# Block 1's loads in another order, attention's last product for two query tiles at a time, and the last tile's norm on VectorE

## The chip, the cores and the metric

The kernel runs on one core of one Trainium2 chip. The metric is the time of one execution in device microseconds (us). A core has TensorE (PE: matrix products; PEld is its loading of weights), VectorE (DVE), ScalarE (ACT), GpSimd (POOL) and SyncE (SP), which here issues all DMAs. Each engine runs its own instructions in the order in which they were written, and waits for others by semaphores. Products are summed up in PSUM, which has 8 banks of 128 x 512 fp32.

## The reference

One decoder layer for 512 positions of width 1024, in fp32, with a condition vector c. All of it is computed:

```python
c_act = silu(c)
sh1, sc1, g1, sh2, sc2, g2 = split(c_act @ ada_w + ada_b, 6)
h = x * (1 + sc1) + sh1
q, k, v, z, xbc, dt = split(h @ w_in, ...)       # w_in 1024 x 4112
o_attn = attention of 8 heads x 64, causal, with a distance penalty
xs, B, C = split(silu(conv4(xbc)))
y = state space scan of 16 heads x 64, gated by silu(z), normed in 2 groups
x = layer_norm(alpha * x + (1 + g1) * (concat(o_attn, y) @ w_out))
h = x * (1 + sc2) + sh2
x = layer_norm(alpha * x + (1 + g2) * conv_ffn(h))   # 1024 -> 2 x 2816 -> 1024
```

## The kernel before

**Precision.** A large product is made of three products of fp32r parts: a tensor `w` is split into a rounded part `wh` (ACT copies it) and the rest `wl` (DVE subtracts), and h into `hh` and `hl`; then wh·hh, wl·hh and wh·hl are summed up in one bank. So for each 512 KB slab `raw` of weights there is one ACT step of 128x1024 (`wh`) and one DVE step (`wl`), and 24 PE products of 512 columns for a tile `fm` (8 blocks of 128 input columns x 3).

**Order of the work.** The kernel is written as some dozens of generators ("threads") with priorities. A planner (class `Order`) takes, step by step, the thread whose next operation could start first by modelled prices, and writes it to its engine. Buffers come from pools with quotas (`buf`, `bank`, `R.limit`); a thread that finds no buffer, or whose `Need(...)` is not marked, stands back. So a change in one thread moves operations of others on all engines. Almost all operations are recorded at line 300 of the profile, inside the planner; the names of tiles tell them apart.

**The start.** h is made in eight blocks of 128 columns (k = 0 to 7). `start_load` issues, on SP, for each block the 256 KB of x (`xk`), a slab of w_in (`wr`, 384 KB) and the columns of ada_w that give the block's shift and scale (`aw`, four DMAs of 256 KB). SP's DMAs rotate over eight semaphores, so a ninth waits for the landing of the first. `start_acc` sums aw times silu(c) over the eight kc on DVE, in two halves that are added at the end (`acc`); `start_h` sums that over the partitions with one-column products on PE (`pa`). A few kc can be left to PE instead: KPE says how many, each then one product of `aw` with `csil` for the shift and one for the scale (the trace counts two instructions for each). From `pa` come `mod` (DVE), then `hh` and `hk` (ACT, from the transposed x, `px`) and `hl` (DVE). `products` keeps six banks (`first`) over all eight blocks, 18 products of 512 columns each; until block 0's hh is there it fills PE with products of the identity (`first<-ident`). Behind block 7 stand 16 products `pd`, then the tiles `fm` of q, k, x and v. ACT and DVE take the four-step convolutions of the six `first` banks (`Y`, `BT`, `CT`: ACT one step, DVE three, of 511, 510 and 509 columns), which frees these banks for fm. Next, with the scan's own steps (`pcs`, `pxt`, `pst`, `py`, `pyo` on PE; `xe`, `csb`, `xd`, `st`, `Y` on DVE), comes attention.

**Attention.** `attention(j)` runs for four pairs of heads, j = 0 to 3, and four query tiles of 128, t = 0 to 3. A unit (j, t, i) makes scores `psS` (PE), maximum (`mx`, DVE), exponentials and scaling of `pr` (ACT, DVE), transposes (`pT`, PE) and copies back to pr. `att_pv` then makes, for each tile t, 2(t+1) products `pov` of pr and V in one bank of the pair; each writes 64 of 128 partitions. The buffers pr are four.

**The end.** `ln2` takes the norm of one of four tiles, in parts as the down product's banks `dn` are done: y, XN (DVE), statistics, then 1/sqrt as a POOL `pow` on one column (mv), `center` (subtract the mean, times gain) and the scale step (times 1/sqrt, plus bias), each one DVE operation; `side` does the same for the last 256 columns with ACT and two POOL operations. Each part has its own DMA to the output.

Of the kernel before, what the change touches and what calls it, by code (L numbers as in the profile page):

```python
# [12 lines left out]
OP = mybir.AluOpType  # L13
# [3 lines left out]
P = 128  # L17
SEQ = 512
DM = 1024
NT = SEQ // P  # L20
KC = DM // P
# [383 lines left out]
def layer_kernel(  # L405
# [13 lines left out]
    out2 = out[0]  # L419
# [119 lines left out]
    NF = 768  # L539
    AW, XK, WR, ACC, WF = {}, {}, {}, {}, {}  # L540

    KPE = {0: 2, KC - 1: 4}

    def start_load():
        for k in range(KC):
            c0 = k * P

            def rows():
                xk = yield buf("s", [P, NT, P], "xk")
                yield S.dma_start(xk, x2[:, c0:c0 + P].rearrange("(t p) f -> p t f", p=P))  # L550
                XK[k] = xk
                R.mark(("x", k))
                wr = yield buf("b", [P, NF], "wr", "raw")
                yield S.dma_start(wr, w_in[k * P:(k + 1) * P, 3328:4096])
                WR[k] = wr
                R.mark(("sl", k))

            if k:
                yield from rows()
            aw = AW[k] = yield buf("e", [P, 2, KC, P], "aw")  # L560
            for k0 in (0, 4):
                for s in range(2):
                    yield S.dma_start(aw[:, s, k0:k0 + 4], ada[k0 * P:(k0 + 4) * P, s * DM + c0:s * DM + c0 + P]
                                      .rearrange("(k p) n -> p k n", p=P))
                R.mark(("aw", k, k0))
            if not k:
                yield from rows()
        R.mark("loads")
        WR["dt"] = yield buf("s", [P, KC, 16], "wdr")
        yield S.dma_start(WR["dt"], w_in[:, 4096:4112].rearrange("(k p) n -> p k n", p=P))  # L570
        R.mark("wdr")

    def start_acc():
        yield Need("csil")
        for k in range(KC):
            acc = yield buf("s", [P, 2, 2, P], "acc")
            n = KC - KPE.get(k, 0)
            for kc in range(n):
                if kc % 4 == 0:
                    yield Need(("aw", k, kc))  # L580
                a_, q = acc[:, kc % 2], AW[k][:, :, kc, :]
                if kc < 2:
                    yield V.tensor_scalar(a_, q, csil[:, kc:kc + 1], None, op0=OP.mult)
                else:
                    yield V.scalar_tensor_tensor(a_, q, csil[:, kc:kc + 1], a_, op0=OP.mult, op1=OP.add)
            yield V.tensor_add(acc[:, 0], acc[:, 0], acc[:, 1])
            if n == KC:
                R.free(AW[k])
            ACC[k] = acc
            R.mark(("acc", k))  # L590
# [34 lines left out]
    def start_h():  # L625
        for k in range(KC):
            yield Need(("acc", k), ("aw", k, 4), "ada_b")
            acc, n = ACC[k], KPE.get(k, 0)
            pa = yield bank("mix", "pa")
            for s in range(2):  # L630
                yield T.matmul(pa[:, s:s + 1], acc[:, 0, s], ones[:, 0:1], start=True, stop=not n)
                for kc in range(KC - n, KC):
                    yield T.matmul(pa[:, s:s + 1], AW[k][:, s, kc], csil[:, kc:kc + 1], start=False, stop=kc == KC - 1)
            if n:
                R.free(AW[k])
            R.free(acc)
            mod = yield buf("t", [P, 2], "mod")
            yield V.scalar_tensor_tensor(mod[:, 1:2], pa[:, 1:2], 1.0, adab[:, 8 + k:9 + k], op0=OP.add, op1=OP.add)
            yield V.tensor_add(mod[:, 0:1], pa[:, 0:1], adab[:, k:k + 1])
            R.free(pa)  # L640
            hk = yield buf("s", [P, SEQ], "hk")
            yield Need(("px", k))
            yield A.activation(hh[:, k], PX[k], AF.Identity, bias=mod[:, 0:1], scale=mod[:, 1:2])
            R.mark(("hh", k))
            yield A.activation(hk, PX[k], AF.Identity, bias=mod[:, 0:1], scale=mod[:, 1:2])
            R.free(PX[k], mod)
            R.mark(("hk", k))
            yield V.tensor_sub(hl[:, k], hk, hh[:, k].bitcast(F32))
            R.free(hk)
            R.mark(("h", k))  # L650
# [314 lines left out]
                R.spawn(att_unit(j, t, i), 4)  # L965

    def att_pv(j, po):
        for t in range(NT):
            yield Need(("pT", j, t, 0), ("pT", j, t, 1))
            yield [T.matmul(po[i * 64:i * 64 + 64, t * P:(t + 1) * P],  # L970
                            VT[b // 2][:, b % 2, (2 * j + i) * 64:(2 * j + i + 1) * 64],
                            PRT[j, t][:, i, b * P:(b + 1) * P], start=(b == 0), stop=(b == t))
                   for b in range(t + 1) for i in range(2)]
            R.free(PRT.pop((j, t)))
        if j % 2 == 0:
            OA[j] = yield buf("e", [P, 2, 2, SEQ], "oa", dt=F32R)
        o = OA[j - j % 2][:, j % 2]
# [281 lines left out]
    def ln2(t, ps, cuts):  # L1259
# [28 lines left out]
        def center(c0, c1):  # L1288
            return V.scalar_tensor_tensor(r[:, c0:c1], r[:, c0:c1], mv[:, 0:1], lg2[:, c0:c1],
                                          op0=OP.subtract, op1=OP.mult)  # L1290

        yield center(*cut[0])
        yield V.scalar_tensor_tensor(mv[:, 3:4], mv[:, 0:1], -1.0, mv[:, 2:3], op0=OP.mult, op1=OP.mult)
        R.spawn(side(cut[-1][1]), 0)
# [292 lines left out]
```

## Time and profile before

| | |
|---|---|
| median of 3 runs | 733.77 us (732.68 to 734.45) |
| profiled execution | 734.33 us, its span 732.6 us |
| PE busy | 717.2 us (98%), granted clock 0.989 on the mean |
| DVE, ACT, POOL busy | 526.4 us (72%), 316.6 us (43%), 60.3 us (8%) |
| bytes read and written | 96.20 MB and 2.13 MB |

The profile tells of one execution: for each engine what it ran and when, and what released it from a wait. The span runs from its first to its last instruction, the rest of the execution's time lies around it. A time like 62.92 is counted from the span's start. In a timeline, PE's duration column holds a modelled pipeline end and is longer than a product's share; the distance of two starts is what a product costs.

### The profile page before, as it was taken

How to read it: one execution, taken by the hardware profiler on the slowest of the kernel's cores; microseconds unless marked ns; L12 is line 12 of the kernel's file. 1: busy time of each engine (PE TensorE's matmuls, PEld its weight loads, DVE VectorE, ACT ScalarE, POOL GpSimd, SP SyncE). 2: the span in 40 equal slices, each digit the busy share in tenths (PEclk: the TensorE clock that was granted, in tenths of full speed). 3: DMA queues.
4: the chain of work that ended last, by engine and by line, in shares of the span. 5: the costliest groups of instructions: out<-in, count | busy, mean ns of one | idle time of the engine just before them, and what ended most of it. 6: DMA issues, size and time to landing. Idle time of an engine off the chain costs nothing.

```text
span 732.6 us, 9614 instructions
## 1 busy us (share of the span) xinstructions
PE 717.2 (98%) x3623; PEld 585.3 (80%) x3623; DVE 526.4 (72%) x929; ACT 316.6 (43%) x526; POOL 60.3 (8%) x70
## 2 busy tenths in 40 slices
PE   8999999999999999999999999999999999999995
PEld 8777777788777788888998888888888888888884
DVE  4888999999898999776865887655656664227246
ACT  2436576663576633332753444444444452212100
POOL 0010102000000001000100000000000009300023
PEclk8999999999999999999999999999999999999998
DMA  9995487453254755232633543332333144323202
GB/s 255 299 258 172 120 231 220 136 165 92 56 167 121 244 210 176 75 101 85 173 88 114 165 152 91 109 88 87 97 105 87 60 159 168 102 87 90 83 30 86
DMA packets 115831, 98.95 MB, mean 135 GB/s; under 512 B 5325, under 2 KB 97865, under 8 KB 115785
## 3 DMA queue, kind: packets, MB, share of 16 engines
q1 hardware_dynamic: 115785, 98.34, 45.1%
q8 instruction: 28, 0.46, 0.3%
q14 instruction: 18, 0.15, 0.1%
HBM read 96.20 MB, written 2.13 MB: 134 GB/s over the span
## 4 chain that ended last, share of the span: by engine, by line
PE 82%; DMA 6%; DVE 6%; ACT 3%; SPq 1%; issue 1%; POOL 1%; POOLq 0%; ACTq 0%; DVEq 0%
PE up L300 34%; PE dn L300 17%; PE fm L300 12%; PE po L300 9%; PE first L300 3%; DMA csb<-drcs 2%; SPq L300 1%; ACT csb L300 1%; PE psS L300 1%; PE pov L300 1%; DMA raw<-in_mix_in_w_dram 1%; PE pT L300 1%; DVE acc L300 1%; DMA aw<-in_ada_w_dram 1%; DVE wl L300 1%
## 5 line engine op out<-in xcount | busy, mean ns | idle before, releaser
L300 DVE TENSOR_TENSOR wl<-raw,wh 128x1024 fp32r<-128x1024 f32 x102 | 128.0, 1256 | 88.7 <-ACT wh L300 86.0
L300 ACT ACTIVATE wh<-raw 128x1024 fp32r<-128x1024 f32 x102 | 106.8, 1051 | 88.3 <-PE dn L300 54.6
L300 PE MATMUL up<-h2h,wh 128*128 128x512 f32 (+1 forms) x384 | 144.7, 377 | 0.0
L300 PE MATMUL up<-h2l,wh 128*128 128x512 f32 (+1 forms) x384 | 144.0, 375 | 0.0
L300 PE MATMUL up<-h2h,wl 128*128 128x512 f32 (+1 forms) x384 | 143.9, 375 | 0.0
L300 PE MATMUL dn<-wh,mid 128*128 128x512 f32 (+1 forms) x356 | 102.5, 371 | 0.0
L300 DVE SCALAR_TENSOR_TENSOR u<-up,fprm,u 128x511 f32<-128x511 f32 x88 | 65.8, 749 | 35.4 <-ACT u L300 33.9
L300 PEld LDWEIGHTS up<-h2h,wl 128*128 128x128 f32 x384 | 72.2, 188 | 14.7
L300 PEld LDWEIGHTS up<-h2h,wh 128*128 128x128 f32 x384 | 72.1, 188 | 14.1
L300 PEld LDWEIGHTS up<-h2l,wh 128*128 128x128 f32 x384 | 72.1, 188 | 14.0
L300 PEld LDWEIGHTS dn<-wh,mid 128*128 128x128 f32 x356 | 64.6, 188 | 12.6
L300 PE MATMUL fm<-hh,wh 128*128 128x512 f32 x176 | 73.9, 420 | 0.0
L300 PE MATMUL fm<-hl,wh 128*128 128x512 f32 x176 | 69.3, 394 | 0.0
L300 PE MATMUL fm<-hh,wl 128*128 128x512 f32 x176 | 69.3, 394 | 0.0
L300 PE MATMUL dn<-wl,mid 128*128 128x512 f32 (+1 forms) x178 | 66.1, 371 | 0.0
L300 ACT ACTIVATE u<-up,fprm 128x512 f32<-128x512 f32 x44 | 34.2, 778 | 51.3 <-PE up L300 51.3
L300 POOL TENSOR_TENSOR XN<-XN,l 128x512 f32<-128x512 f32 x16 | 25.0, 1580 | 244.5 <-ACT l L300 243.8
L300 PE MATMUL po<-wh,os 128*128 128x512 f32 x128 | 41.7, 394 | 0.0
L300 PEld LDWEIGHTS fm<-hh,wl 128*128 128x128 f32 x176 | 33.1, 188 | 7.9
L300 PEld LDWEIGHTS fm<-hh,wh 128*128 128x128 f32 x176 | 33.2, 188 | 7.7 <-issue 1.7
L300 PEld LDWEIGHTS dn<-wl,mid 128*128 128x128 f32 x178 | 33.5, 188 | 6.3
L300 DVE SCALAR_TENSOR_TENSOR acc<-ad,csil,acc 128x1024 f32<-128x1024 f32 x28 | 36.7, 1309 | 2.3 <-DMA ad<-in_ada_w_dram 2.2
(227 smaller groups left out, 1069.2 us busy)
## 6 DMA issues: line engine op xcount, KB each, us to landing
raw<-in_ffn_up_w_dram SPq DMA_DIRECT2D x44, 512.0 KB, 4.4
ad<-in_ada_w_dram SPq DMA_DIRECT2D x32, 512.0 KB, 4.8
raw<-in_mix_in_w_dram SPq DMA_DIRECT2D x26, 512.0 KB, 6.1
raw<-in_ffn_down_w_dram SPq DMA_DIRECT2D x22, 512.0 KB, 4.0
aw<-in_ada_w_dram SPq DMA_DIRECT2D x32, 256.0 KB, 5.9
raw<-in_mix_out_w_dram SPq DMA_DIRECT2D x12, 512.0 KB
csb<-drcs SPq DMA_DIRECT2D x8, 512.0 KB, 5.5
wr<-in_mix_in_w_dram SPq DMA_DIRECT2D x8, 384.0 KB
```

What stands on the lines that cost most here:

```text
L300: getattr(self.hw[op.eng], op.fn)(*op.args, **op.kw)
```

## The change

It has three parts. The first: in `start_load`, block 1's `xk` and `wr` are issued behind its `aw` and no longer ahead of it (block 0 had that order already); and of the kc that PE took, the four of block 7 go to DVE, so that only block 0 leaves two to PE. The second: `att_pv` waits for two query tiles, issues the products of both in one group and frees both buffers behind it. The third: `ln2` of the last tile makes its three parts (512, 256 and 256 columns) on DVE, all three `center` steps and then the three scale steps with a DMA behind each; ACT's and POOL's steps of `side` and the DVE operation that made mv's fourth column are left out there.

```diff
-    KPE = {0: 2, KC - 1: 4}
+    KPE = 2
@@ start_load
-            if k:
+            if k > 1:
                 yield from rows()
...
-            if not k:
+            if k < 2:
                 yield from rows()
@@ start_acc
-            n = KC - KPE.get(k, 0)
+            n = KC - KPE if k == 0 else KC
@@ start_h
-            acc, n = ACC[k], KPE.get(k, 0)
+            acc, n = ACC[k], 0 if k else KPE
@@ att_pv
-        for t in range(NT):
-            yield Need(("pT", j, t, 0), ("pT", j, t, 1))
+        for t0 in range(0, NT, 2):
+            ts = (t0, t0 + 1)
+            yield Need(*(("pT", j, t, i) for t in ts for i in range(2)))
             yield [T.matmul(po[i * 64:i * 64 + 64, t * P:(t + 1) * P],
...
-                   for b in range(t + 1) for i in range(2)]
-            R.free(PRT.pop((j, t)))
+                   for t in ts for b in range(t + 1) for i in range(2)]
+            R.free(*(PRT.pop((j, t)) for t in ts))
@@ ln2
+        if last:
+            cut = cuts
+            for c in cut:
+                yield center(*c)
+            for c0, c1 in cut:
+                q = r[:, c0:c1]
+                yield V.scalar_tensor_tensor(q, q, mv[:, 2:3], lb2[:, c0:c1], op0=OP.mult, op1=OP.add)
+                yield S.dma_start(out2[t * P:(t + 1) * P, c0:c1], q)
+            R.free(mv)
+            return
```

The planner moves other operations with these, on all engines, from the start to the middle of the output projection; behind it the orders are the same until the last tile. Three places follow, each as it stands in before and behind the change. The numbers in the names count buffers and differ between the two.

SP at the start, from the first DMA on; aw_98 is block 0's, xk_121, wr_128 and aw_132 are block 1's in before, aw_121, xk_139 and wr_144 behind the change:

```order
 L300 DMA xk_111<-in_x_dram 128x4x128
 L300 DMA wr_117<-in_mix_in_w_dram 128x768
-L300 DMA xk_121<-in_x_dram 128x4x128
-L300 DMA wr_128<-in_mix_in_w_dram 128x768
-L300 DMA aw_132<-in_ada_w_dram 128x4x128 x4
+L300 DMA aw_121<-in_ada_w_dram 128x4x128 x4
+L300 DMA xk_139<-in_x_dram 128x4x128
+L300 DMA wr_144<-in_mix_in_w_dram 128x768
```

The four aw DMAs moved ahead of the x and the slab of the same block; all other DMAs of the start stand as they stood.

DVE behind block 7, in before: hl of block 7, the first four wl, and the convolutions; first_102 is the bank that BT frees:

```order
L300 TENSOR_TENSOR hl_95<-hk_601,hh_94 128x512
L300 TENSOR_TENSOR wl_609<-raw_390,wh_608 128x1024
L300 TENSOR_TENSOR wl_622<-raw_439,wh_621 128x1024
L300 TENSOR_TENSOR wl_633<-raw_488,wh_632 128x1024
L300 TENSOR_TENSOR wl_659<-raw_535,wh_658 128x1024
L300 SCALAR_TENSOR_TENSOR Y_657<-first_99,prm_76,Y_657 128x511
L300 SCALAR_TENSOR_TENSOR BT_654<-first_102,prm_76,BT_654 128x511
L300 SCALAR_TENSOR_TENSOR BT_654<-first_102,prm_76,BT_654 128x510
L300 SCALAR_TENSOR_TENSOR BT_654<-first_102,prm_76,BT_654 128x509
```

and behind the change:

```order
L300 TENSOR_TENSOR hl_95<-hk_606,hh_94 128x512
L300 TENSOR_TENSOR wl_612<-raw_391,wh_611 128x1024
L300 TENSOR_TENSOR wl_625<-raw_437,wh_624 128x1024
L300 TENSOR_TENSOR wl_636<-raw_486,wh_635 128x1024
L300 SCALAR_TENSOR_TENSOR BT_648<-first_102,prm_76,BT_648 128x511
L300 SCALAR_TENSOR_TENSOR BT_648<-first_102,prm_76,BT_648 128x510
L300 SCALAR_TENSOR_TENSOR BT_648<-first_102,prm_76,BT_648 128x509
```

The fourth wl and the step of Y moved behind BT's three steps (the fourth wl by some 20 rows); on ACT the fourth wh moved likewise, behind the first steps of Y, BT and CT.

PE in the first head pair's attention, in before, from the transposes of tile 0's second head on (pT and pov of pr_1367 are tile 0's, of pr_1368 tile 1's):

```order
L300 MATMUL pT_1429<-ident_68,pr_1367 128x128
L300 MATMUL fm_1353<-hh_94,wh_1076 128x512
L300 MATMUL fm_1353<-hl_95,wh_1076 128x512
L300 MATMUL fm_1353<-hh_94,wl_1077 128x512
L300 MATMUL pT_1442<-ident_68,pr_1368 128x128 x2
L300 MATMUL pf_1444<-ident_68,fr_1428 128x96
L300 MATMUL pov_1366<-pr_1367,V_1351 64x128 x2
L300 MATMUL fm_1353<-hh_94,wh_1076 128x512
...
L300 MATMUL pov_1366<-pr_1368,V_1351 64x128 x4
L300 MATMUL psS_1492<-qk_767 128x512
```

and behind the change (pr_1334 is tile 0's, pr_1335 tile 1's):

```order
L300 MATMUL pT_1462<-ident_68,pr_1335 128x128 x2
L300 MATMUL fm_1445<-hh_94,wh_1105 128x512
L300 MATMUL fm_1445<-hl_95,wh_1105 128x512
L300 MATMUL fm_1445<-hh_94,wl_1106 128x512
L300 MATMUL pT_1472<-ident_68,pr_1336 128x128 x3
L300 MATMUL pov_1333<-pr_1334,V_1317 64x128 x2
L300 MATMUL pov_1333<-pr_1335,V_1317 64x128 x4
L300 MATMUL pT_1475<-ident_68,pr_1336 128x128 x3
```

The products of both tiles stand side by side, behind tile 1's last transposes. Over the whole kernel the groups of pov fall from 16 to 8.

## Rows read from the trace of the kernel before

**Rows 1.** The page: busy time, share of the span and instructions of each engine; and the chain of work that ended last, by engine.

```profile
PE 717.2 (98%) x3623; PEld 585.3 (80%) x3623; DVE 526.4 (72%) x929; ACT 316.6 (43%) x526; POOL 60.3 (8%) x70
PE 82%; DMA 6%; DVE 6%; ACT 3%; SPq 1%; issue 1%; POOL 1%; POOLq 0%; ACTq 0%; DVEq 0%
```

**Rows 2.** Busy time in six stretches. The columns: stretch, its length, busy us and instructions of each engine, the granted clock of PE (1.00 is 2.4 GHz), DMA share, GB/s.

```profile
17.00:50.00 33.00, 31.57 (x153) 25.01 (x151) 28.86 (x77) 13.13 (x18) 0.00 (x0) 1.00 1.09 289
50.00:62.00 12.00, 11.99 (x58) 10.03 (x59) 6.87 (x14) 6.64 (x10) 2.50 (x12) 0.86 0.99 286
62.00:138.00 76.00, 73.45 (x408) 57.12 (x407) 71.24 (x138) 49.55 (x118) 9.71 (x9) 1.00 0.57 162
138.00:262.00 124.00, 123.64 (x765) 97.58 (x765) 113.80 (x279) 72.65 (x153) 4.75 (x8) 1.00 0.49 152
262.00:724.00 462.00, 462.00 (x2175) 381.72 (x2173) 293.46 (x395) 169.33 (x222) 39.41 (x31) 1.00 0.35 107
724.00:732.60 8.60, 0.11 (x1) 0.00 (x0) 4.37 (x10) 0.60 (x1) 3.23 (x4) 0.69 0.28 102
```

**Rows 3.** PE's waits between 58 and 724 us, three of six kinds: who waited, for whom, us in total, times, longest.

```profile
PE py L300 <- ACT csb L300: 0.6, 1, 0.6
PE pst L300 <- DVE xe L300: 0.6, 2, 0.4
PE pT L300 <- DVE pr L300: 0.5, 1, 0.5
```

**Rows 4.** Timeline of PE at the start: start, duration, operation, count.

```profile
11.99 4.19 PE L300 MATMUL first<-ident 128*128 128x128 f32 x18
15.97 1.06 PE L300 MATMUL px<-ident,xk 128*128 128x128 f32 x4
16.68 1.89 PE L300 MATMUL first<-hh,whf 128*128 128x512 f32 x6
18.40 1.53 PE L300 MATMUL first<-hh,wlf 128*128 128x512 f32 x6
```

**Rows 5.** Timeline around blocks 6 and 7: a DVE row, then PE from the second eight one-column products on.

```profile
49.52 0.88 DVE L300 SCALAR_TENSOR_TENSOR acc<-aw,csil,acc 128x256 f32<-128x256 f32 x2
...
52.73 1.03 PE L300 MATMUL pa<-csil,aw 128*128 128x1 f32 x8
53.62 0.94 PE L300 MATMUL first<-hh,whf 128*128 128x512 f32 x3
54.40 2.44 PE L300 MATMUL first<-hh,wlf 128*128 128x512 f32 x6
...
58.75 1.56 PE L300 MATMUL first<-hh,whf 128*128 128x512 f32 x6
60.14 1.53 PE L300 MATMUL first<-hh,wlf 128*128 128x512 f32 x6
...
62.92 0.39 PE L300 MATMUL pd<-hh,wdt 128*32 128x512 f32 x1
```

**Rows 6.** Timeline behind block 7: ACT, then DVE, then PE's first fm.

```profile
59.15 1.06 ACT L300 ACTIVATE wh<-raw 128x1024 fp32r<-128x1024 f32 x1 [0.75 <-DMA raw<-in_mix_in_w_dram]
...
61.99 0.78 ACT L300 ACTIVATE Y<-first,prm 128x512 f32<-128x512 f32 x1
62.67 0.77 ACT L300 ACTIVATE BT<-first,prm 128x512 f32<-128x512 f32 x1
...
60.24 1.23 DVE L300 TENSOR_TENSOR wl<-raw,wh 128x1024 fp32r<-128x1024 f32 x1 [0.59 <-ACT wh L300]
62.02 1.23 DVE L300 TENSOR_TENSOR wl<-raw,wh 128x1024 fp32r<-128x1024 f32 x1 [0.56 <-ACT wh L300]
63.16 0.75 DVE L300 SCALAR_TENSOR_TENSOR Y<-first,prm,Y 128x511 f32<-128x511 f32 x1
63.82 2.31 DVE L300 SCALAR_TENSOR_TENSOR BT<-first,prm,BT 128x511 f32<-128x511 f32 x3
...
66.60 0.39 PE L300 MATMUL fm<-hh,wh 128*128 128x512 f32 x1
```

**Rows 7.** Timeline of PE around two groups of pov, of the first head pair's tiles 0 and 1.

```profile
138.99 0.44 PE L300 MATMUL pov<-pr,V 128*64 128x128 f32 x4
139.36 0.50 PE L300 MATMUL fm<-hh,wh 128*128 128x512 f32 x1
139.70 0.39 PE L300 MATMUL fm<-hl,wh 128*128 128x512 f32 x1
...
141.54 0.40 PE L300 MATMUL fm<-hh,wl 128*128 128x512 f32 x1
141.87 0.66 PE L300 MATMUL pov<-pr,V 128*64 128x128 f32 x8
142.46 0.50 PE L300 MATMUL psS<-qk 128*128 128x512 f32 x1
```

**Rows 8.** Timeline of the tail: DVE, then POOL.

```profile
725.87 0.74 DVE L300 SCALAR_TENSOR_TENSOR XN<-XN,mv,RW 128x512 f32<-128x512 f32 x1
...
727.79 1.34 DVE L300 SCALAR_TENSOR_TENSOR XN<-XN,mv,RW 128x256 f32<-128x256 f32 x2
...
726.03 0.99 POOL L300 TENSOR_TENSOR mv<-mv,half 128x1 f32<-128x1 f32 x1 [1.50 <-DVE mv L300]
727.93 1.79 POOL L300 TENSOR_TENSOR XN<-XN,RW 128x256 f32<-128x256 f32 x2 [0.91 <-ACT XN L300]
```

## The prediction

> **What bounds the kernel now.** I read the page first, then the stretches, then PE's waits, then the timelines of the places that the change touches. [rows 1]: PE is busy 98% of the span and holds 82% of the chain that ended last, so on the whole only what shortens PE's work, or lets PE start it earlier, is worth anything. [rows 2] shows where that is not the whole story. From 262 to 724 PE is busy in all 462.00 us, and what arrives earlier there leaves earlier by as much. From 138 to 262 it is busy 123.64 of 124.00 us, with DVE at 92%. From 62 to 138 PE is busy 73.45 of 76.00 us and DVE 71.24 of 76.00 (94%): two engines near their ends, and the one gains nothing without the other. [rows 3] lists waits of PE after 58 us; three kinds of 0.5 to 0.6 us, all on the chains of DVE and ACT in that stretch. The last 8.6 us have no PE work but one matmul: a chain on DVE, POOL and the output's DMA. Only this tail, PE's path until 62 us and the switches of PE in attention are what the change can move.
>
> **Part 1, the order of the loads and the last block's sums.** *Block 1.* In before, PE makes 18 filler products (11.99 to 15.97), then block 1's transposition, and starts block 0 at 16.68 [rows 4]. Behind the change 14 of these products stand there (7 pairs in place of 9), and the transposition comes after the seventh product of block 0. 14 x 0.221 = 3.1, so block 0 starts at 15.1, 1.6 us earlier. This is an upper end: the first six products of block 0 take 1.72 us (16.68 to 18.40), 287 ns each, where the last 12 of block 7 take 231 [rows 5]: the clock comes back to full in them, and a start while it is low wins slow work. I take 0.4 to 1.2 us at block 1. The blocks behind it are paced by DMA and by DVE as before, and keep no more than that.
>
> *Block 7.* Its four DVE products more (128x256, two took 0.88 us, so 1.8 us) stand where DVE had gaps; I expect its modulation at about 53.5, before PE needs it. PE loses 16 one-column products: eight took 0.89 us (52.73 to 53.62), so 1.8 us go [rows 5]. Behind them 12 products took 4.35 us (54.40 to 58.75) where the last 12 of block 7 took 2.77 (60.14 to 62.92). The granted clock is 0.86 on the mean from 50 to 62 and 1.00 from 17 to 50, where no block has these products [rows 2]: it fell from 2.4 to 1.2 GHz once, behind them. If it stays high, 1.6 us go too. So PE would end block 7 some 0.5 + 1.8 + 1.6 = 3.9 us earlier, at 59.0 in place of 62.9.
>
> *What is late next.* pd takes 3.7 us (62.92 to 66.60), to 62.7. Then stands q's first product, fm, whose bank comes free when DVE has read it in the convolution BT. That is not early by 3.9 us. ACT's third wh waits for its raw slab (59.15, 0.75 us idle on the DMA) and DVE's third wl follows at 60.24 [rows 6]; DMA is at 0.99 of its time there and the bytes are the same, so these stay. In before the fourth wh, the fourth wl (62.02) and a step of Y (63.16) stand between them and BT (63.82 to 66.13, three steps at 0.77). Behind the change these three stand later: ACT goes from wh (ends 60.2) through one step for Y and one for BT, at a pitch of 0.67 each, to 61.6, and DVE's three BT steps end at 61.6 + 2.3 = 63.9. PE starts fm at about 64.2 in place of 66.60: **2.4 us**, whether the clock stays high or not (with 1.6 more on block 7, pd ends at 64.3). PE waits some 1.5 us there.
>
> *Given back until 138.* The DVE steps that free banks and make the weights of q to v stand, with their durations added up along the two orders, up to 2 us of DVE work earlier than before, and PE's steps that wait for DVE (pcs, pxt, pst, py) stand 3 to 12 fm products of 0.233 later, which is 0.7 to 2.8 us of cover. DVE itself can gain only what it idles: 76.00 - 71.24 = 4.8 us, in which part is between instructions. The price lies between -0.6 (one of the waits of [rows 3] goes) and +2.4 (all is lost). I take 0.9 lost, nearer to the lower end because of that cover. Left: **1.5 us**.
>
> **Part 2, two query tiles in one group.** A switch to pov and back costs PE time that is no product [rows 7]. The fm product ahead of a group starts 0.33 us before it (141.54 to 141.87), where products of that size stand 0.23 apart (12 in 2.77 us, [rows 5]); the one behind takes 0.34 (139.36 to 139.70). Four products take 0.37 us, eight 0.59, so each 0.055 and the first 0.15 more. Sum 0.10 + 0.11 + 0.15 = 0.36 a group; where a transposition stands beside it, which has a switch of its own, less: I take 0.31. 16 groups become 8: 8 x 0.31 = 2.5 us. Nothing of it is hidden: PE has 0.36 us idle in 124. The wait becomes longer, since the first tile's products stand behind the second tile's softmax as well; what fills it is fm, which stands in the order between the two tiles' transpositions. Two prob buffers come free together and later, of four, so the next head pair's first scores may start later on DVE. Bounds: 2.9 (all at 0.36) and a loss, as a rival below. I take **2.4 us**.
>
> The Trainium skill, "TensorEngine Tiling (Array Packing)", section Key Properties, has it that changing the tiling mode, and not just the tile, drains TensorE. By that rule the two tiles' products, which alternate between two column halves, cost nothing inside one group, and the sum would be 2.9; a rule by which each half is a switch would make the merge worth less than 0.1. The rows' 0.055 per product agree with the first.
>
> **Part 3, the last tile.** In before, the last output waits for POOL's two steps (727.93, 1.79 us) behind ACT, so it is issued at 729.7 [rows 8]. Behind the change DVE runs from 725.87: three steps for the centre, three for the scale, 512 columns at 0.66 and 256 at 0.48. 2 x (0.66 + 0.48 + 0.48) = 3.24, to 729.1, and pow (to 727.02) is ready before the scales at 727.5. That is 0.6 earlier. The two 256-column steps that ran beside POOL took 1.34 together; at 0.67 each all four would make it 729.9, 0.2 later. POOL is idle in the new scales, so I take **0.4 us** gained. The first store's transfers hide as before; only the last, which has as many bytes as before, stands behind it.
>
> **Sum.** 1.5 + 2.4 + 0.4 = 4.3 us. On the profiled execution's own time, 734.33 (its span is 732.6, and 1.7 lie around it), that is 730.0; its time is 0.56 above the median of the runs, 733.77, against which the forecast is **729.5**.
>
> **The rivals.** A measurement of this kernel tells 0.2% (1.5 us) from no change, so faster is below 732.3 and slower above 735.2.
> *B, DVE takes the start back.* PE comes 2.4 us earlier at q, and finds pst, py and the first scores no earlier, since DVE is busy 94% from 62 to 138. For it: three waits of PE in [rows 3] are already of this kind. Against it: PE's order has those steps later. Left: 2.4 + 0.4, so 731.0.
> *C, more.* The waits in [rows 3] go (1.7) and nothing is given back (0.9): 729.5 - 2.6 = 726.9.
> *D, the saved time is spent.* As B, and the longer wait for the second tile costs as much as the switches: left is the tail, 733.4. A form of it: PE's wait at 62.7 lets the clock fall to half once more, which by the stretch 54.40 to 58.75 costs 1.6. The Trainium skill, "TensorE: Matmul & The Clock Gate", section What's actually happening, says that the throttled state is the default and activity releases it. By it, this wait is a risk that the sum leaves out; the profile shows waits of 0.5 to 0.7 us with full clock from 62 on, and none as long as 1.5.
> *E, slower.* Place: the eight pair groups. If at each PE stands for the second tile's DVE chain (for each of two heads a wait like the 0.5 of pT on pr in [rows 3]), that is 8 x 1.0 = 8.0 us: 729.5 + 8.0 = 737.5. From 4.3 / 8 = 0.54 us a pair on, nothing is left of the gain. Against it: fm products stand in the order between a pair's transpositions and its group.
>
> **How the numbers follow.** Forecast 0.48 (728 to 730.5 its own range), B 0.18, C 0.08, D 0.15, E 0.11. A, B and C are faster: 0.74; D is no change: 0.15; E is slower: 0.11. The range leaves out E and half of C: 726.8 to 733.4.
>
> **What would show it.** Right: block 7's products at one pace and full clock from 50 to 62; BT ending near 63.9 and fm starting near 64.2; eight pov groups; PE's last matmul near 720; the last store near 0.4 us closer behind it. Wrong: fm still at 66 or later (then wl or wh holds BT); PE waits on xe, csb or pr that are together over 2.4 us longer between 62 and 138 (B); PE waiting for pr ahead of each pov group (E); a low clock behind 62.7 (D).

## The result and the profile after

The changed kernel takes 730.84 us (median of 10 runs, 728.20 to 732.63), where the kernel before took 734.62 in the same sitting (10 runs, 732.68 to 737.05). The recorded ratio, over all runs of both, is 0.9946, with an interval of 0.9929 to 0.9964 (the two medians alone give 0.9949, 3.8 us). On 734.62 that is 4.0 us less, within an interval of 2.6 to 5.2. The forecast was 4.3 us less.

The profiled execution took 731.86 us, its span is 730.2 us. The page's busy time by engine and the chain that ended last, by engine [rows 1]:

```profile
PE 711.8 (97%) x3603; PEld 579.8 (79%) x3603; DVE 528.8 (72%) x931; ACT 315.6 (43%) x528; POOL 57.7 (8%) x68
...
PE 79%; DVE 7%; DMA 5%; SPq 5%; ACT 2%; issue 2%; POOL 1%; DVEq 0%; POOLq 0%; ACTq 0%
```

PE lost 5.4 us of its busy time, which is more than the span lost (2.4), and its share of the chain went from 82% to 79%; DVE has 7% (6%) and SP's queue 5% (1%). PE has become a little less the bound. Three of the first stretches, two of them those of [rows 2] (busy time of PE, PEld, DVE, ACT and POOL, then the granted clock, the DMA share and GB/s):

```profile
0.00:17.00 17.00, 13.41 (x79) 11.80 (x79) 8.61 (x25) 4.81 (x7) 0.74 (x7) 1.00 0.91 255
...
50.00:62.00 12.00, 11.92 (x53) 8.21 (x54) 8.20 (x16) 7.28 (x11) 2.55 (x12) 1.00 1.02 292
62.00:138.00 76.00, 72.44 (x402) 58.15 (x401) 70.93 (x146) 46.77 (x113) 7.64 (x8) 0.98 0.55 154
```

From 50 to 62 the clock is full now (0.86 in before). From 62 to 138 PE idles 3.6 us in place of 2.5, and there the clock is no longer full: 0.98. The three largest of PE's waits in the trace after, from 58 to 720 (us in total, times, longest), which answer to [rows 3]:

```profile
PE py L300 <- DVE csb L300: 1.9, 1, 1.9
PE fm L300 <- DVE BT L300: 1.3, 1, 1.3
PE pst L300 <- DVE xe L300: 0.4, 1, 0.4
```

Two are new or longer: the first product of q, which the prediction named, and py, which it had at 0.6. PE's timeline of the start and of block 7, from the start to q's first product [rows 4, 5]:

```profile
13.48 1.65 PE L300 MATMUL first<-hh,whf 128*128 128x512 f32 x6 [0.73 <-ACT hh L300]
...
48.51 0.97 PE L300 MATMUL first<-hh,whf 128*128 128x512 f32 x3 [0.49 <-ACT hh L300]
50.01 0.94 PE L300 MATMUL first<-hh,whf 128*128 128x512 f32 x3
...
54.29 1.66 PE L300 MATMUL first<-hh,whf 128*128 128x512 f32 x6
55.78 1.55 PE L300 MATMUL first<-hh,wlf 128*128 128x512 f32 x6
57.17 1.56 PE L300 MATMUL first<-hl,whf 128*128 128x512 f32 x6
58.57 0.39 PE L300 MATMUL pd<-hh,wdt 128*32 128x512 f32 x1
...
63.70 0.47 PE L300 MATMUL fm<-hh,wh 128*128 128x512 f32 x1 [1.29 <-DVE BT L300]
```

Block 7 ends at 58.57 (62.92 in before), all its products at one pace. q's first product is ready to go at 62.4 and waits until 63.70. What it waits for [rows 6]: first ACT's timeline behind block 7,

```profile
58.74 1.06 ACT L300 ACTIVATE wh<-raw 128x1024 fp32r<-128x1024 f32 x1 [0.74 <-DMA raw<-in_mix_in_w_dram]
...
60.37 0.77 ACT L300 ACTIVATE BT<-first,prm 128x512 f32<-128x512 f32 x1
```

and DVE's:

```profile
59.83 1.23 DVE L300 TENSOR_TENSOR wl<-raw,wh 128x1024 fp32r<-128x1024 f32 x1 [0.57 <-ACT wh L300]
61.24 2.32 DVE L300 SCALAR_TENSOR_TENSOR BT<-first,prm,BT 128x511 f32<-128x511 f32 x3 [0.18 <-ACT BT L300]
```

The third wl still stands ahead and still waits, over ACT, for its slab; ACT's step of BT stands behind the third wh, and DVE's steps of BT follow it after 0.18 us. BT ends at 63.56, which is 61.24 + 2.32.

One attention group of the first head pairs, two tiles at a time [rows 7], from PE's timeline:

```profile
200.01 0.88 PE L300 MATMUL pov<-pr,V 128*64 128x128 f32 x12
200.82 0.55 PE L300 MATMUL pT<-ident,pr 128*128 128x128 f32 x3
```

Twelve instructions take 0.81 us (200.01 to 200.82); 0.15 + 12 x 0.055, by the prediction's prices, is 0.81. They are six products: for pov, as for the one-column products, the trace counts two instructions to a product, and the prediction's numbers of both, and those below, are the trace's. The end [rows 8], from the timeline of all engines:

```profile
721.93 0.28 PE L300 MATMUL dn<-wh,mid 128*128 128x256 f32 x1
...
723.97 2.99 DVE L300 SCALAR_TENSOR_TENSOR XN<-XN,mv,RW 128x512 f32<-128x512 f32 x6
724.13 0.99 POOL L300 TENSOR_TENSOR mv<-mv,half 128x1 f32<-128x1 f32 x1 [1.51 <-DVE mv L300]
...
726.19 1.31 SPq L300 DMA_DIRECT2D out_dram<-XN  x3
```

The six steps take 2.99 us in one row and pow, ready at 725.12, holds up none of them. From the start of the last matmul to the span's end it is 730.2 - 721.93 = 8.3 us; in before its last matmul starts at 723.83, 8.8 before the end.

### The profile page after: what moved, and what is told of

It reads as the page before. It is cut to its first block, busy times and chain, and to the rows that moved or that the text cites. A ratio compares the mean times of both kernels' runs of the same rounds, so it can differ in the third digit from the quotient of the medians.

```text
span 730.2 us, 9572 instructions
## 1 busy us (share of the span) xinstructions
PE 711.8 (97%) x3603; PEld 579.8 (79%) x3603; DVE 528.8 (72%) x931; ACT 315.6 (43%) x528; POOL 57.7 (8%) x68
## 4 chain that ended last, share of the span: by engine, by line
PE 79%; DVE 7%; DMA 5%; SPq 5%; ACT 2%; issue 2%; POOL 1%; DVEq 0%; POOLq 0%; ACTq 0%
PE up L300 34%; PE dn L300 17%; PE fm L300 13%; PE po L300 7%; SPq L300 5%; DMA aw<-in_ada_w_dram 2%; DMA csb<-drcs 1%; PE tm L300 1%; PE psS L300 1%; DVE Y L300 1%; PE pov L300 1%; DMA raw<-in_mix_in_w_dram 1%; PE pT L300 1%; ACT csb L300 1%; DVE acc L300 1%
```

## The experiments

**The theory and its rivals.** The theory is the prediction's: each part takes away what its step says, and a part of what the start wins is given back where PE meets the pace of DVE. The first rival is that more is given back (B): then the parts are worth more alone than together, and an earlier q brings nothing. The second is that part 1's gain isn't the order of the loads at all, but block 7's 16 products. The third is that the clock decides (the form of D). Each expectation says in its own words what its theories are.

The twelve runs below were made in three sittings on three chips, each beside the kernel before. The ratio is the recorded one to the kernel before in the same sitting (it lies within 0.0006 of the ratio of the medians):

| run | ratio | interval | us less |
|---|---|---|---|
| p1_start_only | 0.9953 | 0.9934 to 0.9971 | 3.5 |
| p2_pov_only | 0.9963 | 0.9949 to 0.9976 | 2.7 |
| p3_tail_only | 0.9991 | 0.9980 to 1.0002 | 0.7 |
| p1o_load_order_only | 0.9983 | 0.9973 to 0.9994 | 1.2 |
| p1k_block7_on_dve_only | 0.9950 | 0.9935 to 0.9965 | 3.7 |
| p23_without_start | 0.9958 | 0.9945 to 0.9970 | 3.1 |
| a_after_again | 0.9943 | 0.9926 to 0.9960 | 4.2 |
| m_bt_before_third_wl | 0.9950 | 0.9931 to 0.9969 | 3.7 |
| m_py_later | 1.0142 | 1.0122 to 1.0163 | -10.4 |
| m_pov_four_tiles | 0.9873 | 0.9854 to 0.9892 | 9.3 |
| b4_four_tiles_only | 0.9947 | 0.9930 to 0.9965 | 3.9 |
| c4_four_tiles_old_loads | 0.9897 | 0.9882 to 0.9912 | 7.6 |

The profiled execution of each gives PE's place at five points that all the kernels have: when the first product of block 0 starts, the first of block 6, the first pd (block 7's end), q's first product, and the first up (from it on the orders are the same). "after again" is the second execution of the changed kernel (a_after_again). Times are the starts in PE's timeline, in us from the span's start; the clock is the granted clock of the stretch.

| run | loads | 16 products of block 7 | pov groups | clock 0 to 17 | block 0 | block 6 | clock 50 to 62 | pd | q | up |
|---|---|---|---|---|---|---|---|---|---|---|
| before | old | kept | 16 | 0.81 | 16.68 | 50.01 | 0.86 | 62.92 | 66.60 | 353.58 |
| p3 | old | kept | 16 | 0.83 | 16.69 | 50.36 | 0.86 | 63.25 | 66.93 | 354.26 |
| p2 | old | kept | 8 | 1.00 | 13.77 | 48.41 | 0.86 | 61.88 | 65.78 | 349.57 |
| p23 | old | kept | 8 | 0.90 | 15.24 | 48.80 | 0.72 | 63.56 | 67.25 | 351.78 |
| b4 | old | kept | 4 | 1.00 | 13.56 | 46.84 | 0.86 | 59.73 | 63.42 | 348.59 |
| p1k | old | gone | 16 | 0.81 | 16.06 | 49.62 | 1.00 | 59.48 | 63.17 | 349.31 |
| c4 | old | gone | 4 | 0.90 | 15.30 | 48.30 | 1.00 | 58.14 | 61.83 | 347.97 |
| p1o | new | kept | 16 | 0.90 | 13.73 | 48.59 | 1.00 | 59.92 | 65.09 | 352.76 |
| p1 | new | gone | 16 | 1.00 | 13.29 | 47.46 | 1.00 | 57.47 | 62.36 | 349.51 |
| after | new | gone | 8 | 1.00 | 13.48 | 48.51 | 1.00 | 58.57 | 63.70 | 351.07 |
| after again | new | gone | 8 | 1.00 | 13.20 | 48.08 | 1.00 | 58.10 | 63.00 | 348.09 |
| m_bt | new | gone | 8 | 0.90 | 13.94 | 48.58 | 1.00 | 58.77 | 62.45 | 350.42 |
| m_py | new | gone | 8 | 0.90 | 13.58 | 47.01 | 1.00 | 56.85 | 61.37 | 365.78 |
| m_pov4 | new | gone | 4 | 0.80 | 15.79 | 49.02 | 1.00 | 58.86 | 62.54 | 345.00 |

### The three parts, each alone

Part 1 alone is the change without the new `att_pv` and `ln2`:

```diff
-    KPE = {0: 2, KC - 1: 4}
+    KPE = {0: 2}
...
-            if k:
+            if k > 1:
...
-            if not k:
+            if k < 2:
```

> The first part of the change alone (block 1's loads in the new order, block 7's four kc on VectorE); attention and tail as before. Theory S (the start wins 2.4 to 2.9 us at q's first fm, because the third wl and BT set it, and the stretch to 138 gives part of it back): fm starts near 63.9, the time is 1.0 to 2.0 us below before. Rival (the start's gain is all given back where PE waits for DVE): fm near 63.9 too, but the time within 0.5 us of before. Rival (the gain comes from block 7's products alone and reaches the end): 3 us or more below.

Measured: 3.5 us less (2.1 to 4.8). That is above theory S's 1.0 to 2.0 and where the last rival has it. q starts at 62.36, earlier than expected, after a wait of 1.0 for BT, and py waits 2.0 for csb:

```profile
PE py L300 <- DVE csb L300: 2.0, 1, 2.0
PE fm L300 <- DVE BT L300: 1.0, 1, 1.0
```

Part 2 alone:

```diff
-        for t in range(NT):
+        for t0 in range(0, NT, 2):
+            ts = (t0, t0 + 1)
...
```

> The second part alone: attention's products for two query tiles in one group. Theory P (a switch of PE to pov and back costs 0.31 us, eight are saved, and PE is the bound there): 2.0 to 2.5 us below before, PE's waits between 138 and 262 as before. Rival (the longer wait for the second tile costs what the switches cost): within 0.7 us of before, with waits of PE on pr or kl grown by 1.5 us or more.

Measured: 2.7 us less (1.8 to 3.7). PE's waits in that trace:

```profile
PE pst L300 <- DVE xe L300: 0.7, 2, 0.4
PE py L300 <- ACT csb L300: 0.6, 1, 0.6
PE pT L300 <- DVE pr L300: 0.5, 1, 0.5
```

These are the kinds of [rows 3]; the only new kind is pcs on dd, 0.3 us. From 138 to 262 PE is busy all 124.00 us: the longer wait for the second tile's softmax is covered by other products. Rival E, with its 1.0 us a pair, falls.

Part 3 alone:

```diff
+        if last:
+            cut = cuts
...
+            R.free(mv)
+            return
```

> The third part alone: the last tile's norm on VectorE. Theory T (the last store is issued when DVE is done and no longer when POOL is): from PE's last matmul to the end of the span 0.4 to 0.6 us less than before's 8.6, nothing else moved; time 0.5 us below, inside the noise. Rival (stores pace the tail): 8.5 to 8.6 us as before.

Measured: 0.7 us less, in an interval that reaches from 1.5 less to 0.1 more. By the trace the tail is 732.7 - 724.51 = 8.2 us long, 0.6 shorter; the ratio alone would not have shown it.

This trace serves as a second one of the kernel before, since up to the last tile nothing is changed. Its q starts at 66.93 and its first up at 354.26 (66.60 and 353.58 in before), but its py waits longer:

```profile
PE py L300 <- ACT csb L300: 1.9, 1, 1.9
```

In before it is 0.6. The chain ahead of it is late in p3: GpSimd's step on csb, which waits there for csb's DMA, starts at 88.62 (87.92 in before), ACT's behind it at 90.09 (89.05), and py at 97.71 (96.66). So a wait of this length comes without the change too, and the clock stays at 1.00 behind it (96 to 106).

### Part 1 taken apart

The new order of the loads, with block 7's products kept on PE (KPE as in before):

```diff
-            if k:
+            if k > 1:
...
-            if not k:
+            if k < 2:
```

> Of the first part only the order of block 1's loads; block 7 keeps its 16 one-column products on PE. Theory S: block 7 ends 0.3 to 1.0 us earlier than 62.9, the low clock behind the one-column products stays, fm starts with the end of pd near 65.8, and the time is 0 to 0.8 us below before. Rival (the load order is what frees PE, the products of block 7 are hidden): fm near 64 and the time as of the first part alone.

Measured: 1.2 us less (0.4 to 2.0). The 16 products are still there, but the clock stays full behind them, which theory S did not expect. PE's timeline:

```profile
49.86 0.71 PE L300 MATMUL first<-hh,whf 128*128 128x512 f32 x2
...
50.63 1.03 PE L300 MATMUL pa<-csil,aw 128*128 128x1 f32 x8
...
51.75 1.03 PE L300 MATMUL pa<-csil,aw 128*128 128x1 f32 x8
...
52.96 1.56 PE L300 MATMUL first<-hh,wlf 128*128 128x512 f32 x6
```

Two products of 512 columns, of block 6, stand here between the transposition and the one-column products; in the five kernels whose clock falls, none does. Whether that decides it was not tested. In this trace pd comes 3.0 us earlier than in before, but q, which waits 1.3 for BT, only 1.5.

The other half, block 7's four kc on DVE, with the old order of the loads:

```diff
-    KPE = {0: 2, KC - 1: 4}
+    KPE = {0: 2}
```

> Of the first part only block 7's four kc on VectorE; the loads in the order of before. Theory S: what part 1 is worth comes mostly from here: the 16 one-column products (1.8 us) and the low clock behind them (1.6 us) go, PE's end of block 7 is 3 us or more earlier than 62.9, fm starts near 64 when BT stands ahead of the fourth wl, and the time is 1.5 to 3 us below before. Rival (VectorE's 1.8 us more delay block 7's modulation when the loads are not earlier): PE waits at block 7 and the time is within 0.7 us of before.

Measured: 3.7 us less (2.6 to 4.8), more than theory S's 1.5 to 3 and no less than all of part 1. q starts at 63.17 without a wait, and the clock is full.

The table tells the size of each term. From block 6's start to pd, the eight traces without the products take 9.84 to 10.19 us, 9.96 on the mean. p1o, the one trace with them and a full clock, takes 11.33: the products cost 1.4. The kernels with them and the old loads take 12.89, 12.89, 12.91, 13.47 and 14.76: the fall of the clock costs 1.6 in three, 2.1 in p2 and 3.4 in p23 (clock 0.72). What block 6's start gains by the loads is 0.7 us, from 48.91 on the mean (46.84 to 50.36, seven kernels) to 48.18 (47.01 to 49.02, seven); the two ranges overlap for the most part. So the second rival is right to a large part: part 1 is mostly block 7's products and what the clock does behind them.

### Where is the saved time held up?

If q's start decides, it should help to let BT free its bank before the third wh and wl, which are what held BT in the trace after:

```diff
@@ w_split
             yield Need(("raw", i))
+            if i == 2:
+                yield Need(("freed", 9))
@@ conv4
         R.free(ps)
+        R.mark(("freed", ch))
```

> The changed kernel, with the third wh and wl held back until BT's bank is free. Theory S (the third wl, behind its slab's DMA, sets when BT ends): BT ends near 62.3, fm starts with the end of pd near 62.3 and not at 63.7, PE's wait on BT (1.3 us) is gone. Whether the time follows: if PE alone bounds the stretch to 138, 1.3 us below the changed kernel (729.5 beside its 730.8); if VectorE takes it back, as it took back the start's gain, within 0.5 us of it.

Measured: 3.7 us less than before (2.3 to 5.1), as the change itself. BT ends at 61.65 and q starts at 62.45 right behind pd, with no wait. But PE's waits are now:

```profile
PE pcs L300 <- DVE dd L300: 2.4, 1, 2.4
PE py L300 <- issue: 1.0, 1, 1.0
```

The wait moved from q to pcs, which needs dd from DVE, and grew. The mechanism of rival B is real at this margin: an earlier q, with the DVE work in an order that does not serve the next step, is given back. (py's wait on csb is 0.6 here: the edit moved the scan's steps too.)

The wait of py on csb, 1.9 us, is the longest of the trace after. To hold py back in PE's order, the planner's margin (0.35 in its start estimates) was raised to 2.0 for the scan's output steps, until the last of its early states is done:

```diff
                 margin = self.MARGIN if ops[0].eng == "PE" and rank[0] < 9 else 0.0
+                if ops[0].eng == "PE" and th.gen.__name__ == "ssd_out" and ("ssd", 6) not in self.done:
+                    margin = 2.0
```

> The changed kernel, with the first products py of the scan placed some nine products of 0.233 us later in PE's order (the planner is told to keep 2.0 us distance from their inputs until the first of these threads is done). Theory G (what part 1 wins is given back in one place, where PE waits 1.9 us for csb inside py, with the clock low behind it for 1.6 us in the profiled execution): no wait on csb over 0.7 us, clock 1.00 from 96 to 106, and 1.9 to 3.5 us below the changed kernel. Rival (VectorE and ScalarE are late as a whole there): the wait stands at the next py or pst, and the time is within 0.7 us of the changed kernel.

Measured: 10.4 us more (8.9 to 12.0). PE's waits:

```profile
PE pad L300 <- DVE accl L300: 7.7, 1, 7.7
PE pst L300 <- DVE xe L300: 2.7, 1, 2.7
PE psS L300 <- ACT V L300: 2.4, 1, 2.4
```

The wait of py is gone, and three others came, the largest one ahead of the feed-forward, where DVE makes the last sum of the second modulation (accl) too late. The edit moved far more than py, so it is no test of what the wait on csb costs.

The same kernel as after, in another sitting, for the spread of its profile:

```diff
(no line differs)
```

> The changed kernel itself once more, for a second trace beside the same runs of before. Parts 1, 2 and 3 alone gave 3.4, 2.7 and 0.7 us, 6.8 in all, and together 3.9. Theory O (the order that the planner finds for all three has waits of its own, inside py and at 173 to 189 us): the waits of 0.4 us and more between pd and up are again 4.5 us or more, whether or not the clock falls behind py. Theory L (the clock that fell behind py in the profiled execution is what is missing): clock 1.00 from 96 to 106 and a time near 728, or the clock low again and a time near 731.

Measured: 4.2 us less (2.9 to 5.4), as in the first sitting. The waits of 0.4 us and more come to 3.4 us (py 1.9, fm 1.1, psS 0.4), below theory O's 4.5; the clock is 1.00 from 96 to 106, and this execution took 728.92, near theory L's 728, while the median of the six is 729.97. The profiled execution has a span of 727.2 us, 3.0 less than the other one. PE's timeline there, behind the wait on csb:

```profile
99.90 0.66 PE L300 MATMUL py<-csb,xd 128*64 128x128 f32 x8 [1.89 <-DVE csb L300]
100.49 0.50 PE L300 MATMUL tm<-wh,hh 128*128 128x512 f32 x1
100.83 0.39 PE L300 MATMUL tm<-wl,hh 128*128 128x512 f32 x1
101.06 0.40 PE L300 MATMUL tm<-wh,hl 128*128 128x512 f32 x1
...
102.78 1.12 PE L300 MATMUL py<-csb,xd 128*64 128x128 f32 x16
```

And in the first execution:

```profile
100.61 0.66 PE L300 MATMUL py<-csb,xd 128*64 128x128 f32 x8 [1.90 <-DVE csb L300]
101.19 0.75 PE L300 MATMUL tm<-wh,hh 128*128 128x512 f32 x1
101.74 0.63 PE L300 MATMUL tm<-wl,hh 128*128 128x512 f32 x1
102.16 0.63 PE L300 MATMUL tm<-wh,hl 128*128 128x512 f32 x1
...
105.04 1.09 PE L300 MATMUL py<-csb,xd 128*64 128x128 f32 x16
```

The wait is the same to 0.01 us. Behind it the starts stand 0.23 apart in the one and 0.43 in the other: the clock fell to half there, from 2.4 to 1.2 GHz. From the py behind the wait to the next py it is 4.43 us against 2.88, so the fall costs 1.55 us. The windows of the first execution say the same (columns as above):

```profile
96.00:101.00 5.00, 3.10 (x26) 2.21 (x24) 4.93 (x7) 4.97 (x14) 0.00 (x0) 1.00 0.81 213
101.00:105.00 4.00, 4.00 (x15) 2.82 (x10) 3.68 (x7) 3.27 (x8) 0.00 (x0) 0.57 0.57 159
```

In the first 5 us PE works 3.10 and DVE 4.93: what PE waits for is DVE, which has no gap. DVE's timeline shows what stood ahead of csb: three steps of a convolution.

```profile
97.55 2.31 DVE L300 SCALAR_TENSOR_TENSOR Y<-fm,prm,Y 128x511 f32<-128x511 f32 x3
99.78 1.28 DVE L300 TENSOR_TENSOR csb<-csb,sc 128x512 f32<-128x512 f32 x2
```

### Do the parts add up?

The change without part 1 (`KPE` and the loads as in before; the two lines that read `KPE` go back as well and are left out here):

```diff
-    KPE = 2
+    KPE = {0: 2, KC - 1: 4}
...
-            if k > 1:
+            if k:
...
-            if k < 2:
+            if not k:
...
```

> The changed kernel without its first part (the start as before; attention in pairs of tiles, and the tail). If the parts add up, 3.3 us below before (731), which leaves 0.5 for the start beside them; if the start is worth its 3.4 in this company too, this kernel is at 734.

Measured: 3.1 us less (2.2 to 4.0), which is what parts 2 and 3 give alone (2.7 + 0.7). So part 1 adds only 4.1 - 3.1 = 1.0 us to them (4.1 is the mean of the change's two sittings), where it gives 3.5 alone. All three alone sum up to 6.8; with the intervals of the three as independent, that is uncertain by 1.9, and 4.1 by 0.9. So 2.7 us are missing, uncertain by 2.1.

Two causes come to mind, and the numbers speak against both as the whole of it. Waits: part 1 alone has the waits of py (2.0) and q (1.0) that the change has (1.9 and 1.3, in the second trace 1.9 and 1.1), and keeps its 3.5. Clock: the mean granted clock over all runs is 0.994 for part 1 alone, and 0.995 and 0.996 for the change in its two sittings. What is missing in company stays open.

### Fewer groups still

Four tiles in one group, on top of the change:

```diff
-        for t0 in range(0, NT, 2):
-            ts = (t0, t0 + 1)
+        for t0 in range(0, NT, 4):
+            ts = range(t0, t0 + 4)
```

> The changed kernel, with all four query tiles of a head pair in one group of products: 4 groups in place of 8. Theory P (a group costs 0.3 us of switches): 1.0 to 1.3 us below the changed kernel. Rival (all four prob buffers are held until the last tile is done, so the next head pair waits): PE waits on pr, kl or mx 2 us or more between 138 and 262, and the time is 1 us or more above the changed kernel.

Measured: 9.3 us less than before (7.9 to 10.7), 724.53 us, the fastest kernel of this study. One group and what follows it, from PE's timeline:

```profile
168.39 2.41 PE L300 MATMUL pov<-pr,V 128*64 128x128 f32 x40
170.72 0.94 PE L300 MATMUL pyo<-CT,st 128*128 128x128 f32 x6
```

40 instructions (20 products) take 2.33 us; 0.15 + 40 x 0.055 = 2.35. PE's longest wait:

```profile
PE py L300 <- DVE csb L300: 1.6, 1, 1.6
```

There is no wait of q (62.54 follows pd at once) and no fall of the clock behind py. Only four groups less than after, at 0.31, would be 1.2 us; it won 5.3. To tell the groups from the rest, four tiles on the kernel before:

```diff
-        for t in range(NT):
-            yield Need(("pT", j, t, 0), ("pT", j, t, 1))
+        for t0 in range(0, NT, 4):
+            ts = range(t0, t0 + 4)
+            yield Need(*(("pT", j, t, i) for t in ts for i in range(2)))
...
```

> The kernel before with only one edit: all four tiles of a head pair in one group of products (16 groups become 4). By the switches alone 12 x 0.3 = 3.6 us below before. If the 5.3 us that four tiles gained over two tiles came from fewer waits in the scan and not from attention, this kernel shows 3 to 4 and its waits between pd and up are those of before (3.3 us); if the four-tile order as such is worth more, 6 or more.

Measured: 3.9 us less (2.6 to 5.1); twelve groups less at 0.31 are 3.7. Its waits come to 3.4 us, as before's 3.3 expected, but 2.0 of them are py's, with the clock low behind it. And the change with four tiles, but the old order of the loads:

```diff
-            if k > 1:
+            if k:
...
-            if k < 2:
+            if not k:
...
-        for t0 in range(0, NT, 2):
-            ts = (t0, t0 + 1)
+        for t0 in range(0, NT, 4):
+            ts = range(t0, t0 + 4)
```

> The changed kernel with four tiles in a group and with block 1's loads in the order of before. Theory S (block 7's products are what part 1 is worth, as its half alone gave 3.6 of 3.4 us, the load order nothing): as the four-tile kernel with the new loads, 724.5, within 1 us. Rival: 1 us or more slower.

Measured: 7.6 us less (6.5 to 8.7). The loads are worth 1.7 in this company, uncertain by 1.8: that is on the rival's side, but does not tell it from theory S. With four tiles, part 1 is worth 9.3 - 3.9 - 0.7 = 4.7 us, uncertain by 2.0, so here it is not lost. Of the 5.3 us that four tiles win over two, 1.2 is the groups; by these sums the rest is that part 1's gain arrives. What makes the planner's order pass it on with four tiles and not with two was not taken apart.

## Why the prediction was right

The sum was 4.3 us and 4.0 was measured (4.2 in the other sitting). Its terms, with the differences to before in the two profiled executions of the changed kernel (first, second):

| | forecast | first | second |
|---|---|---|---|
| block 7's end, first pd | -3.9 | -4.4 | -4.8 |
| q's first product | -2.4 | -2.9 | -3.6 |
| first up: the above, less what is given back, and the groups' 2.4 | -3.9 | -2.5 | -5.5 |
| last matmul | -3.9 | -1.9 | -4.9 |
| span's end, with the tail | -4.3 | -2.4 | -5.4 |

At the end the first execution stands 1.9 us short of the forecast and the second 1.1 beyond it; their mean, 3.9, is near the 4.0 of all runs.

*Block 0 and 1.* The prediction had 15.1 for block 0 and took 0.5 of it to block 7. Block 0 started at 13.48 and 13.20. But that is not the change alone: p2 and b4 start as the kernel before does and had 13.77 and 13.56 at a full clock, and the four-tile kernel, with the new loads, had 15.79 at 0.80. In the table the start goes by the clock more than by the order: the 18 filler products that took 3.98 us in before (0.221 each, the price that the prediction used for the 14) took 2.08 in p2, at full clock. At block 6 the mean gain was 0.7, in ranges that overlap for the most part, so the 0.5 agrees but is not shown, and its working (four filler products fewer) was one cause of several.

*Block 7.* Right in kind, and 3.0 in place of 3.4 in size: the products are 1.4 (by one trace) and not 1.8, the clock 1.6 as taken. The prediction put the clock's fall down to the products alone. p1o speaks against that: it keeps them, and the clock stays full. All five traces with the products and the old loads show the fall, and none of the nine others does; what the old loads add to it stays open.

*What is late next.* Named rightly, and to half a us: BT's end at 63.56 (63.9), q at 63.70 (64.2), PE's wait 1.3 and 1.1 (1.5). The reason was the one given, that the third wl waits for its slab, though the slab did not quite stay: ACT's third wh starts at 58.74 and 58.03 (59.15 in before). m_bt shows that this wait is no loss that could be had back by itself: with it gone the time is the same.

*Given back.* From q to the first up, before takes 286.98 us. With 2.5 taken off for eight groups, the change gives back 2.9 in the first execution (287.37) and 0.6 in the second (285.09); the forecast was 0.9, its bounds -0.6 and 2.4, which the first execution leaves. Of the 2.3 us between the two, 1.55 is the clock behind py's wait: the form of D that the prediction priced at 1.6, at a wait that it did not name. Without it the first gives back 1.4. The prediction saw that PE's waits on DVE's scan steps could grow, but counted on the 0.7 to 2.8 us of fm products that the new order puts ahead of them; py's wait is 1.9 in spite of these, in place of 0.6. But p3 has 1.9 in the order of before, so the one trace of before set too low a mark, and how much of this wait is the change's doing is not shown.

The Trainium skill, "TensorE: Matmul & The Clock Gate", section What's actually happening, has the throttled state as the default that activity releases. The first execution agrees (1.00 until 101, then 0.57 until 105, behind 1.90 us of waiting); the second, with 1.89, does not show it.

*The groups.* Right: 2.4 forecast, 2.7 measured alone (1.8 to 3.7), and 3.9 for twelve groups. E falls, since in p2 and in the change no wait on pr became longer than the 0.5 of before. That the two halves' products alternate freely inside a group holds for 40 instructions as well (2.33 us), as the Trainium skill's "TensorEngine Tiling (Array Packing)", section Key Properties, would have it.

*The tail.* 0.5 in place of 0.4: the last 256-column steps ran at the pace of the undisturbed ones, as argued.

*Where it may have been lucky.* For part 1 the sum had 1.5 us. Beside parts 2 and 3 it is worth 1.0, uncertain by 1.3, which agrees; alone it is worth 3.5, and with four tiles 4.7. So the sum came out for this company, but "given back" is not confirmed as a general price: part 1 alone gives back next to nothing by its trace (q to the first up 287.15, before 286.98), with the same two waits. And the sum had 2.4 at q less 0.9, where the two traces have 3.3 less 1.8 on the mean: both terms were too small, and that the misses cancel to the same 1.5 is luck.

*The last half us.* From the first up to the last matmul before takes 370.25 us and the changed kernel 370.86 and 370.87, with PE busy throughout and the same order. The prediction had no term for this, and no run explains it: part 1 and part 2 alone take 369.98 and 369.95. It is not one execution's: p3 takes 370.25 as before does.

## What to carry to other kernels

When a start is shortened, follow the earlier work to the next step that another engine or a load paces, and count only what is early there: here 4.6 us at block 7's end were 3.3 at the next bank. Small products on another tile of PE (128*64 between 128*128 here) are worth putting in fewer groups, at some 0.3 us a group, as long as other work stands in the order to fill the longer wait. Where a planner writes the order, try a change's parts alone and in company, since one more step of the same edit (four tiles in place of two) can be worth four times its own price.

## What the hardware showed

The same wait of PE (1.90 and 1.89 us, at the same place of the same program) was followed by half clock in one execution and by full clock in the other. Over the kernels with a wait of py between 1.6 and 2.0 us, the profiles of after, b4 and c4 show the fall (0.83 to 0.87 on the mean from 96 to 106), and those of the second after, p1, p1k, p1o, p3 and m_pov4 don't. So the profile of one execution does not say whether a wait of this length costs 0 or 1.6 us more.

The start of the program differs as much: with the same orders of loads block 0 starts between 13.56 and 16.69, or 13.20 and 15.79, and the granted clock from 0 to 17 is between 0.80 and 1.00. And DMA moved between 277 and 344 GB/s from 50 to 62 us, and the slab that BT's chain waits for goes with it: at 344 (p1), 313 and 292 GB/s (the change's second and first trace) ACT's third wh starts at 57.40, 58.03 and 58.74 and q at 62.36, 63.00 and 63.70, with a wait for BT in all three. A difference of 1 to 3 us at one place of one trace can be the execution's own.
